# Four weight units read with a column step of 2, 4, 8 and 16 in a single-core encoder block

## The chip, the core and the metric

The kernel runs on one core of a Trainium2 chip. The metric is the device time of one execution in microseconds. It was 908.79 us before the change (median of two runs, 908.68 and 908.90).

## What is computed

One encoder block on 256 tokens of width 2048, in float32: a normed input projection into queries, keys, values and Fourier channels, windowed attention and a Fourier mix, an output projection, then a feed-forward part. Only the feed-forward part matters here:

```python
D_FF = ((8 * D_MODEL // 3 + 127) // 128) * 128      # 5504 = 43 tiles of 128
def _conv_ffn(h, w_up, dw_w, dw_b, w_down):
    up = h @ w_up                                   # (256, 2048) @ (2048, 11008)
    gate, val = up[..., :D_FF], up[..., D_FF:]
    gate = lax.conv_general_dilated(gate, dw_w, ...) + dw_b
    act = jax.nn.gelu(gate, approximate=False) * val
    return act @ w_down
```

## The kernel before

The kernel keeps float32 accuracy by writing each operand as the sum of a high and a low part, both in the fp32r format, and adding three products: high x high, low activation x high weight, high activation x low weight. The instruction order of every engine is written out by hand; nothing is rescheduled.

Weights come in *units*. A unit of the up-projection is one tile of 128 output columns, either of the gate or of the value half, over all 16 k tiles of the contraction: an SBUF tile of 128 partitions x 2048 elements, in which k tile k holds columns k*128 to k*128+127. One DMA of 1024 KB brings it (`load`, L183, three raw buffers), and two whole-row instructions split it (`split`): the scalar engine copies the high part (L191) and the vector engine subtracts for the low part (L192). The halves lie in one of three `parts` buffers.

`still_weights` then multiplies a unit. Weights are the stationary operand, so that each matmul has a weight load of 128 x 128 ahead of it (LDWEIGHTS in the profile, under PEld). For each of the 16 k tiles there are two matmuls: at L393 the high weights against the high and low activations, 512 columns, and at L395 the low weights against the high activations, 256 columns. The moving operand is read through `in_turn`, which takes one column from one half of the row and the next from the other half, 256 elements (1024 bytes) away:

```python
def in_turn(ap):
    return ap.rearrange("p (a e) -> p e a", a=2)
```

The main loop runs over `items`, an order fixed at build time. It begins with gate 0, value 0, gate 1, value 1, gate 2, value 2, gate 3, value 3; afterwards gate and value units alternate with products of the down-projection (`by_parts`, L1123 to L1125, matmuls of 512 columns). The last seven tiles are multiplied by `still_thirds` (L406, three matmuls of 256 columns for each k tile). After the two matmuls' sum is in PSUM, the scalar engine copies one half (L901) and the vector engine adds and scales (L902, L904); convolution, GELU and the product with the value follow one or two items later.

Two places in the kernel read SBUF with a step on other engines, and the prediction uses them. Values of late tiles are split with a step of 2 elements (L947 on the scalar engine, L948 on the vector engine, through `by_parity`), and the keys of the attention part with a step of 4 elements (L662 and L663):

```python
keys = add.rearrange("p (r a b) -> p a b r", a=2, b=2)
```

Of the kernel before, what the change touches and what calls it, by code (L numbers as in the profile page):

```python
# [13 lines left out]
P = 128  # L14
D = 2048
S = 256
NK = D // P
# [28 lines left out]
for _g in range(NKV):  # L46
# [21 lines left out]
}  # L68

PATTERNS = ["uuu" + "su" + "suu" * 6] + ["uuu" + "su" * 13 + "s"] * 3  # L70
PATTERNS += ["uuu" + "su" * 11 + "lslslsl"]
# [25 lines left out]
def block_kernel(  # L97
# [18 lines left out]
    nc = tc.nc  # L116
# [13 lines left out]
    def in_turn(ap):  # L130
        return ap.rearrange("p (a e) -> p e a", a=2)
# [17 lines left out]
    items, up_index = ff_items(), {}  # L149

    def in_thirds(j):

        return j >= LATE[0]
# [14 lines left out]
    raws, halves = {}, {}  # L168
# [59 lines left out]
    ps = bank(dn, "ps_warm")  # L228
# [19 lines left out]
    for c in range(4):  # L248
        t = base.tile([P, 4, 512], F32R, tag=f"hT{c}", name=f"hT{c}")
# [42 lines left out]
    k = 0  # L292
# [86 lines left out]
                ps, ah, wl, start=False, stop=last and q == q0 + len(kk) - 1  # L379
            )  # L380

    def still_weights(hi, lo, ps, kk, lag=0):


        todo = [("hi", k) for k in kk[: lag + 1]]
        for n, k in enumerate(kk):
            todo.append(("lo", k))
            todo += [("hi", q) for q in kk[lag + 1 + n : lag + 2 + n]]
        for part, k in todo:
            h = hT[k // 4][:, k % 4, :]  # L390
            s = slice(k * P, (k + 1) * P)
            if part == "hi":
                nc.tensor.matmul(ps, hi[:, s], in_turn(h), start=k == 0, stop=False)  # L393
            else:
                nc.tensor.matmul(  # L395
                    ps[:, 0:S], lo[:, s], in_turn(h)[:, 0:P], start=False, stop=k == NK - 1
                )

    def still_thirds(hi, lo, ps):
# [449 lines left out]
    for n, (c, kq) in enumerate(OUT_ORDER):  # L849
# [15 lines left out]
        if kq >= 2:  # L865
            part = "a" if kq == 2 else "f"
            ps = ps_a[c] if kq < 3 else ps_a[c, "f"]
# [315 lines left out]
    for q in range(2):  # L1183
        kind, j = items[q]
        ps = bank(mm, f"ps_{kind}{j}")
# [16 lines left out]
    for n, it in enumerate(items):  # L1202
        if n < 2:
            continue
        if it[0] == "last":
            break
        if n in (FIRST_PRODUCT - 9, FIRST_PRODUCT - 8):
            ring_load()
        if n == FIRST_PRODUCT - 6:
            pending.append(lambda: first_sums(*SETS[0]))  # L1210
        if it[0] in ("gate", "val"):
            kind, j = it
            ps = bank(mm, f"ps_{kind}{j}")
            if not in_thirds(j):
                still_weights(*halves.pop(up_index[n]), ps, range(NK), lag=4 if n == 2 else 0)
            else:
                still_thirds(*halves.pop(up_index[n]), ps)
            ff_step(n)
            up_posts(n, kind, j, ps)
            continue  # L1220
        if it[0] == "product":
            kind, g, c, p = it
            hi, lo = halves.pop(it)
            both = c == 2
            shape = (2, 1024) if both else (4, 512)
            for cc in (0, 1) if both else (c,):
                o = 512 * cc if both else 0
                if (cc, p) in held:
                    first, end = (g, c) == FIRST_SET[cc], (g, c) == LAST_SET[cc]
                    by_parts(held[cc, p], parts[p], hi, lo, first, end, *shape, o)  # L1230
                    continue
                ps = bank(mm, f"ps_{p}{g}{cc}")
                by_parts(ps, parts[p], hi, lo, True, True, *shape, o)
                at(beside, n + 1, product_out, g, cc, p, ps)
            if (g, c) == LAST_SET.get(c) and p == "P6":
                todo = shared_out(c)
                for m in (1, 3, 5):
                    at(behind, n + m, next, todo, None)
        else:
            kind, g, c = it  # L1240
            hi, lo = halves.pop(up_index[n])
            ps = [bank(mm, f"ps_l{g}{c}{b}") for b in range(2)]
            for b in range(2):
                moving_weights(hi, lo, 512, LATE, act.get, b, ps[b], True, True)
            at(beside, n + 1, down_out, c, ps)
            if (g, c) == (0, 0):
                gfb = base.tile([P, D], F32, tag="hT0", name="gfb")
                nc.gpsimd.dma_start(gfb, normf_g.partition_broadcast(P))
        ff_step(n)
# [53 lines left out]
def _layout(inp):  # L1303

    import numpy as np

    f = lambda a: np.ascontiguousarray(np.asarray(a), dtype=np.float32)
    x = f(inp["x"]).reshape(P, 2, D)
    by_parity = np.arange(S).reshape(P, 2).T.reshape(-1)

    def in_turn(w):

        return f(w).reshape(*w.shape[:-1], -1, 256, 2).swapaxes(-1, -2).reshape(w.shape)

    def tiles(v):
        return f(v).reshape(-1, P).T

    def moving(w, cols):

        return in_turn(w[:, cols]).reshape(-1, 4, P, cols.stop - cols.start).transpose(  # L1320
            0, 2, 1, 3
        ).reshape(-1, P, 4 * (cols.stop - cols.start))

    def still(w, c0):

        return f(w[:, c0 : c0 + P]).reshape(-1, P, P).transpose(1, 0, 2).reshape(1, P, -1)

    w_in = np.asarray(inp["w_in"])
    start = {"q": 0, "k": AW}
    kv = NKV * HD  # L1330
    win = np.concatenate(
        [moving(w_in, slice(AW + kv, AW + 2 * kv))]
        + [still(w_in, start[t] + h * HD) for t, h in QK_ORDER]
    )
    u0 = AW + 2 * kv
    u_rows = np.concatenate(
        [x.transpose(1, 0, 2).reshape(S, NK, P).transpose(2, 1, 0),
         in_turn(w_in[:, u0 : u0 + FW]).reshape(NK, P, FW).transpose(1, 0, 2)], axis=2,
    )
    w_out = np.asarray(inp["w_out"])  # L1340
    wout = np.concatenate(
        [moving(w_out, slice(c * 512, (c + 1) * 512))[k : k + 1] for c, k in OUT_ORDER]
    )
    w_up = np.asarray(inp["w_up"])
    wup = np.concatenate(
        [still(w_up, o + j * P) for j in range(NF) for o in (0, DFF)]
    )
    w_dn = np.asarray(inp["w_down"])
    def rows_by(tiles, cols, width=512):

        w = in_turn(w_dn[tiles[0] * P : (tiles[-1] + 1) * P, cols : cols + width])
        return w.reshape(len(tiles), P, width).transpose(1, 0, 2).reshape(P, -1)

    downs = []
    for g, c in SETS:
        half = len(GROUPS[g]) // 2
        width = 1024 if c == 2 else 512
        for k in (GROUPS[g][0], GROUPS[g][half]):
            for n in (0, 1024):
                downs.append(rows_by(range(k, k + half), n + (0 if c == 2 else 512 * c), width))  # L1360
    late = [rows_by(LATE, 512 * c) for c in range(4)]
    dw = f(inp["dw_w"]).reshape(3, NF, P).transpose(2, 1, 0).reshape(P, 3 * NF)
    sink = np.broadcast_to(f(inp["sink"])[None, :], (P, NH))
    vecs = np.concatenate(
        [tiles(inp["norm1_g"]), tiles(inp["norm2_g"]), tiles(inp["attn_out_g"]),
         tiles(inp["fourier_out_g"]), dw, tiles(inp["dw_b"]), sink], axis=1,
    )
    t = np.arange(S)
    ang = 2.0 * np.pi * ((t[:, None] * t[None, :]) % S) / S
    c_pos = np.concatenate(  # L1370
        [np.cos(ang[:, : S // 2 + 1]), np.sin(ang[:, 1 : S // 2])], axis=1
    )
    c_pos = c_pos[by_parity].reshape(2, P, P, 2).transpose(1, 3, 0, 2)
    k = np.arange(P)
    ang = 2.0 * np.pi * ((k[:, None] * k[None, :]) % P) / P
    c_chan = np.concatenate([np.cos(ang), -np.sin(ang)], axis=1) / np.sqrt(S * P)
    dist = np.abs(t[:, None] - t[None, :]).astype(np.float64)
    c_rel = np.where(dist <= WINDOW, dist, FAR)[by_parity][:, by_parity]
    c_rel = c_rel.reshape(2, P, S).transpose(1, 0, 2)
    return {  # L1380
        "x": x,
        "u_in": np.concatenate([tiles(inp["norm1_g"]), u_rows.reshape(P, -1)], axis=1),
        "vecs": np.ascontiguousarray(vecs),
        "wf": in_turn(f(inp["w_fourier"]).transpose(1, 0, 2).reshape(P, FW)),
        "w_in": win,
        "w_out": wout,
        "w_up": wup,
        "w_down": np.stack(downs),
        "w_down_late": np.stack(late),
        "w_down_last": np.stack([rows_by(LAST, 512 * c) for c in range(4)]),  # L1390
        "normf_g": f(inp["normf_g"]),
        "c_pos": np.ascontiguousarray(c_pos.reshape(P, 2 * S), dtype=np.float32),
        "c_chan": np.ascontiguousarray(c_chan, dtype=np.float32),
        "c_rel": np.ascontiguousarray(c_rel.reshape(P, 2 * S), dtype=np.float32),
    }
# [16 lines left out]
```

## Time and profile before

| | |
|---|---|
| time, median of two runs | 908.79 us |
| the profiled execution, its own time | 908.46 us |
| its span, first to last instruction | 906.7 us |
| TensorE matmul busy | 897.3 us (99%), 5299 instructions |
| TensorE weight load busy | 818.5 us (90%) |
| VectorE busy | 740.8 us (82%) |
| ScalarE busy | 545.6 us (60%) |
| granted TensorE clock | 0.998 |

In the profile PE is the matmul part of the tensor engine and PEld its weight loads, which overlap with the matmuls. Matmul rows overlap each other, since a row's duration includes the passage through the array; how long a matmul occupies the engine is read from the distance between starts. In rows of groups the columns are line, engine, operation, output and inputs, shape and count, then busy time and mean duration, then the idle time before them.

### The profile page before, as it was taken

How to read it: one execution, taken by the hardware profiler on the slowest of the kernel's cores; microseconds unless marked ns; L12 is line 12 of the kernel's file. 1: busy time of each engine (PE TensorE's matmuls, PEld its weight loads, DVE VectorE, ACT ScalarE, POOL GpSimd, SP SyncE). 2: the span in 40 equal slices, each digit the busy share in tenths (PEclk: the TensorE clock that was granted, in tenths of full speed). 3: DMA queues.
4: the chain of work that ended last, by engine and by line, in shares of the span. 5: the costliest groups of instructions: out<-in, count | busy, mean ns of one | idle time of the engine just before them, and what ended most of it. 6: DMA issues, size and time to landing. Idle time of an engine off the chain costs nothing.

```text
span 906.7 us, 13179 instructions
## 1 busy us (share of the span) xinstructions
PE 897.3 (99%) x5299; PEld 818.5 (90%) x5299; DVE 740.8 (82%) x879; ACT 545.6 (60%) x655; POOL 50.3 (6%) x64
## 2 busy tenths in 40 slices
PE   9999999999999999999999999999999999999996
PEld 8899999888899999999999999999999999999985
DVE  7579888676678877879887998888989789889796
ACT  7757777555455655556555575556655556655544
POOL 0001111000000000000000000000000000000003
PEclk9999999999999999999999999999999999999999
DMA  9874544446568687677898779787797978869742
GB/s 360 335 236 142 186 162 164 153 173 232 186 253 264 228 256 251 180 263 227 259 285 276 249 242 297 245 275 237 269 260 246 325 230 279 263 212 266 234 186 93
DMA packets 32765, 214.88 MB, mean 237 GB/s; under 512 B 3616, under 2 KB 3872, under 8 KB 8384
## 3 DMA queue, kind: packets, MB, share of 16 engines
q1 hardware_dynamic: 28592, 184.55, 54.4%
q0 software_dynamic: 4112, 29.49, 17.2%
q8 instruction: 41, 0.67, 0.3%
q14 instruction: 20, 0.16, 0.0%
HBM read 211.93 MB, written 2.10 MB: 236 GB/s over the span
## 4 chain that ended last, share of the span: by engine, by line
PE 90%; DMA 4%; issue 3%; POOL 1%; DVE 1%; ACT 0%; SPq 0%; ACTq 0%; POOLq 0%
PE ps_val L393 14%; PE ps_gate L393 14%; PE ps_gate L395 7%; PE ps_val L395 7%; PE ps_q L393 5%; PE ps_gate L406 4%; PE ps_val L406 4%; PE ps_P L1123 3%; PE ps_P L1125 3%; PE ps_P L1124 3%; PE ps_N L1123 2%; PE ps_N L1125 2%; PE ps_N L1124 2%; PE ps_q L395 2%; PE ps_a L376 2%
## 5 line engine op out<-in xcount | busy, mean ns | idle before, releaser
L192 DVE TENSOR_TENSOR parts<-raw,parts 128x2048 fp32r<-128x2048 f32 (+1 forms) x129 | 293.3, 2273 | 52.4 <-ACT parts L191 51.9
L191 ACT ACTIVATE parts<-raw 128x2048 fp32r<-128x2048 f32 (+1 forms) x129 | 245.5, 1903 | 48.9 <-PE ps_a L378 12.4
L393 PE MATMUL ps_val<-hU,parts 128*128 128x512 f32 x576 | 190.7, 382 | 0.0
L393 PE MATMUL ps_gate<-hU,parts 128*128 128x512 f32 x576 | 190.2, 382 | 0.0
L395 PE MATMUL ps_val<-hU,parts 128*128 128x256 f32 x576 | 157.0, 273 | 0.0
L395 PE MATMUL ps_gate<-hU,parts 128*128 128x256 f32 x576 | 156.4, 273 | 0.0
L393 PEld LDWEIGHTS ps_val<-hU,parts 128*128 128x128 f32 x576 | 108.9, 189 | 15.2
L393 PEld LDWEIGHTS ps_gate<-hU,parts 128*128 128x128 f32 x576 | 108.8, 189 | 15.2
L395 PEld LDWEIGHTS ps_val<-hU,parts 128*128 128x128 f32 x576 | 110.5, 192 | 0.6
L395 PEld LDWEIGHTS ps_gate<-hU,parts 128*128 128x128 f32 x576 | 110.3, 192 | 0.8
L901 ACT ACTIVATE ft_g<-ps_gate 128x256 f32<-128x256 f32 x36 | 13.8, 384 | 98.8 <-PE ps_gate L395 96.2
L393 PE MATMUL ps_q<-hT,parts 128*128 128x512 f32 x192 | 62.6, 384 | 0.0
L1123 PE MATMUL ps_P<-parts_P,op_P 128*128 128x512 f32 x144 | 54.7, 380 | 0.0
L1124 PE MATMUL ps_P<-parts_P,op_P 128*128 128x512 f32 x144 | 54.6, 379 | 0.0
L1125 PE MATMUL ps_P<-parts_P,op_P 128*128 128x512 f32 x144 | 54.6, 379 | 0.0
L901 ACT ACTIVATE ft_v<-ps_val 128x256 f32<-128x256 f32 x36 | 13.8, 384 | 63.1 <-PE ps_val L395 63.1
L395 PE MATMUL ps_q<-hT,parts 128*128 128x256 f32 x192 | 50.4, 273 | 0.0
L1009 DVE TENSOR_TENSOR parts_N<-sumw,parts_N 128x2048 fp32r<-128x2048 f32 x18 | 41.2, 2289 | 10.2 <-ACT parts_N L1008 10.2
L1123 PE MATMUL ps_N<-parts_N,op_N 128*128 128x512 f32 x108 | 41.0, 380 | 0.0
L1124 PE MATMUL ps_N<-parts_N,op_N 128*128 128x512 f32 x108 | 40.9, 379 | 0.0
L1125 PE MATMUL ps_N<-parts_N,op_N 128*128 128x512 f32 x108 | 40.9, 379 | 0.0
L393 PEld LDWEIGHTS ps_q<-hT,parts 128*128 128x128 f32 x192 | 36.1, 189 | 4.7
(350 smaller groups left out, 1707.3 us busy)
## 6 DMA issues: line engine op xcount, KB each, us to landing
raw<-in_w_up SPq DMA_DIRECT2D x86, 1024.0 KB, 6.0
raw<-in_w_in SPq DMA_DIRECT2D x20, 1024.0 KB, 5.9
sumw<-in_w_down POOLq DMA_DIRECT2D x18, 1024.0 KB, 8.6
raw<-in_w_out SPq DMA_DIRECT2D x16, 1024.0 KB, 4.8
raw<-in_w_down_late SPq DMA_DIRECT2D x4, 1024.0 KB, 6.0
u_raw<-in_u_in SPq DMA_DIRECT2D x4, 768.0 KB, 10.4
raw<-in_w_down_last SPq DMA_DIRECT2D x4, 768.0 KB, 4.2
u_raw<-in_u_in SPq DMA_DIRECT2D x7, 384.0 KB, 6.0
```

What stands on the lines that cost most here:

```text
L191: nc.scalar.activation(hi, raw, AF.Copy)
L192: nc.vector.tensor_tensor(lo, raw, f32(hi), ALU.subtract)
L376: nc.tensor.matmul(ps, ah, wh, start=first and q == q0, stop=False)
L393: nc.tensor.matmul(ps, hi[:, s], in_turn(h), start=k == 0, stop=False)
L395: nc.tensor.matmul(ps[:, 0:S], lo[:, s], in_turn(h)[:, 0:P], start=False, stop=k == NK - 1)
L406: nc.tensor.matmul(ps[:, 0:S], w[:, s], in_turn(h)[:, part * P : (part + 1) * P], start=k == 0 and n == 0, stop=k == NK - 1 and n == 2,)
L901: nc.scalar.activation(tmp, ps[:, S : 2 * S], AF.Copy)
L1009: nc.vector.tensor_tensor(lo, src, f32(hi), ALU.subtract)
L1123: nc.tensor.matmul(ps, o[:, 0, p, :], wh, start=first and p == 0, stop=False)
L1124: nc.tensor.matmul(ps, o[:, 1, p, :], wh, start=False, stop=False)
L1125: nc.tensor.matmul(ps, o[:, 0, p, :], wl, start=False, stop=end)
```

## The change

A table `STEPS` names four units and a step for each: gate 2 with 2, value 2 with 4, gate 3 with 8, value 3 with 16. For these units the host lays the columns of `step` neighbouring k tiles out in turn: first column 0 of each of them, then column 1 of each, and so on. `columns` gives a matmul the 128 columns of k tile k as a slice with that step. The values that are multiplied, the order of the products and the size of every transfer are the same; the other 82 gate and value units have step 1. In the changed kernel the two matmuls stand at L401 and L403.

```diff
+STEPS = {("gate", 2): 2, ("val", 2): 4, ("gate", 3): 8, ("val", 3): 16}
...
+    def columns(t, k, step):
+
+        o = k // step * step * P + k % step
+        return t[:, o : o + step * (P - 1) + 1 : step]
+
-    def still_weights(hi, lo, ps, kk, lag=0):
+    def still_weights(hi, lo, ps, kk, lag=0, step=1):
...
         for part, k in todo:
             h = hT[k // 4][:, k % 4, :]
-            s = slice(k * P, (k + 1) * P)
+            w = columns(hi if part == "hi" else lo, k, step)
             if part == "hi":
-                nc.tensor.matmul(ps, hi[:, s], in_turn(h), start=k == 0, stop=False)
+                nc.tensor.matmul(ps, w, in_turn(h), start=k == 0, stop=False)
             else:
                 nc.tensor.matmul(
-                    ps[:, 0:S], lo[:, s], in_turn(h)[:, 0:P], start=False, stop=k == NK - 1
+                    ps[:, 0:S], w, in_turn(h)[:, 0:P], start=False, stop=k == NK - 1
                 )
...
-                still_weights(*halves.pop(up_index[n]), ps, range(NK), lag=4 if n == 2 else 0)
+                still_weights(
+                    *halves.pop(up_index[n]), ps, range(NK), lag=4 if n == 2 else 0,
+                    step=STEPS.get((kind, j), 1),
+                )
...
+    for (kind, j), step in STEPS.items():
+        w = wup[2 * j + (kind == "val")]
+        w[:] = w.reshape(P, -1, step, P).swapaxes(2, 3).reshape(P, -1)
```

## The prediction

> **What bounds the kernel now.** I read the page's busy shares first, then the chain that ended last, then the costliest groups, then the busy time by stretch for the four units that change.
>
> ```profile
> span 906.7 us, 13179 instructions
> PE 897.3 (99%) x5299; PEld 818.5 (90%) x5299; DVE 740.8 (82%) x879; ACT 545.6 (60%) x655; POOL 50.3 (6%) x64
> ...
> PE 90%; DMA 4%; issue 3%; POOL 1%; DVE 1%; ACT 0%; SPq 0%; ACTq 0%; POOLq 0%
> ...
> L393 PE MATMUL ps_gate<-hU,parts 128*128 128x512 f32 x576 | 190.2, 382 | 0.0
> L395 PE MATMUL ps_gate<-hU,parts 128*128 128x256 f32 x576 | 156.4, 273 | 0.0
> L393 PEld LDWEIGHTS ps_gate<-hU,parts 128*128 128x128 f32 x576 | 108.8, 189 | 15.2
> L395 PEld LDWEIGHTS ps_gate<-hU,parts 128*128 128x128 f32 x576 | 110.3, 192 | 0.8
> ```
>
> The tensor engine is the bound and its weight loads are busy beside it almost all the time: the load row of L393 has 15.2 us of idle before it over 576 loads, that of L395 only 0.8. So in a gate or value unit one of the two loads of a k tile is tight. The four units that change are gate 2, value 2, gate 3 and value 3, the fifth to eighth units of the up-projection. They follow one another without a gap:
>
> ```profile
> core 0: us, PE busy (x) PEld busy (x) DVE busy (x) ACT busy (x) POOL busy (x), PEclk, DMA share, GB/s
> 266.94:272.18 5.24, 5.24 (x35) 4.82 (x34) 4.83 (x6) 3.47 (x6) 0.00 (x0) 1.00 1.00 408
> 272.18:277.42 5.24, 5.24 (x35) 4.82 (x34) 4.29 (x6) 2.67 (x3) 0.00 (x0) 1.00 0.75 283
> 277.42:282.66 5.24, 5.24 (x35) 4.82 (x34) 5.21 (x6) 2.61 (x3) 0.94 (x1) 1.00 0.86 245
> 282.66:287.90 5.24, 5.24 (x35) 4.82 (x34) 3.89 (x6) 2.67 (x3) 0.00 (x0) 1.00 0.97 228
> 287.90:500.00 212.10, 212.10 (x1225) 192.87 (x1224) 175.19 (x181) 124.76 (x131) 6.96 (x8) 1.00 0.78 249
> 500.00:700.00 200.00, 200.00 (x1136) 181.28 (x1135) 176.81 (x175) 122.38 (x119) 8.75 (x10) 1.00 0.81 257
> 700.00:890.00 190.00, 190.00 (x1252) 176.75 (x1252) 164.65 (x158) 108.81 (x98) 7.61 (x10) 1.00 0.76 241
> ```
>
> Two things are to be seen. Each unit takes 5.24 us, which is 5.24 / 16 = 327.5 ns for one k tile (one high matmul of 512 columns at L393 and one low matmul of 256 at L395). And from 287.90 to 890.00 the tensor engine never stands still, so there is no later wait that could swallow a delay: what these four units lose arrives at the end in full, and no other engine gets work that it did not have.
>
> Now the inside of a k tile. The matmul rows overlap, so starts are to be compared, not durations:
>
> ```profile
> 500.20 0.38 PE L1123 MATMUL ps_P<-parts_P,op_P 128*128 128x512 f32 x1
> 500.41 0.38 PE L1124 MATMUL ps_P<-parts_P,op_P 128*128 128x512 f32 x1
> 500.63 0.38 PE L1125 MATMUL ps_P<-parts_P,op_P 128*128 128x512 f32 x1
> ...
> 266.94 0.38 PE L393 MATMUL ps_gate<-hU,parts 128*128 128x512 f32 x1
> 267.15 0.27 PE L395 MATMUL ps_gate<-hU,parts 128*128 128x256 f32 x1
> ...
> 266.94 0.19 PEld L395 LDWEIGHTS ps_gate<-hU,parts 128*128 128x128 f32 x1
> 267.16 0.19 PEld L393 LDWEIGHTS ps_gate<-hU,parts 128*128 128x128 f32 x1
> ...
> 764.91 1.31 PEld L406 LDWEIGHTS ps_gate<-hU,parts 128*128 128x128 f32 x11
> ```
>
> A matmul of 512 columns occupies (500.63 - 500.20) / 2 = 215 ns; I take 216. A load starts together with the matmul before the one it serves (266.94 with 266.94, 267.16 with 267.15), so only one load is ahead, and a slot lasts as long as the longer of matmul and load. Eleven loads in a row at L406, behind 256-column matmuls, take 1.31 us: (1310 - 192) / 10 = 112 ns each, of which I call 111.5 the load's occupancy, because 216 + 111.5 gives the 327.5 measured. Hence the model used below, for a load of X ns: one k tile costs max(216, X) + max(111.5, X). The high slot has 104 ns to spare, the low slot none.
>
> **The change part by part.** Removed and added: no instruction. The order of every engine's instructions is the same in number and kind, so no wait, no transfer and no queue moves. The host arranges the four units' columns differently; the transfers stay 1024 KB each, and the split into halves (L191, L192) still reads and writes whole contiguous rows, so its durations stay. These parts cost nothing because nothing in them changes, not because something hides them. What changes is the address pattern of 4 x 32 = 128 weight loads: consecutive columns lie 2, 4, 8 or 16 elements (8, 16, 32, 64 bytes) apart.
>
> The trace has no weight load with a step; the contiguous ones of these lines last 189 and 192 ns (rows above). The nearest rows are the scalar and vector engines' reads of the same memory with steps: L529/L530 contiguous, L947/L948 in steps of 2, L662/L663 in steps of 4 (each with 256 elements).
>
> ```profile
> L275 ACT ACTIVATE parts<-u_raw 128x1024 fp32r<-128x1024 f32 x4 | 4.2, 1044 | 0.0
> L191 ACT ACTIVATE parts<-raw 128x2048 fp32r<-128x2048 f32 x126 | 241.1, 1913 | 40.8 <-PE ps_a L378 12.4 <-PE ps_ff L378 9.1 <-PE ps_P L1125 6.5
> L529 ACT ACTIVATE chan_hl<-chan 128x256 fp32r<-128x256 f32 x1 | 0.4, 407 | 0.0
> L947 ACT ACTIVATE act<-fa_v 128x256 fp32r<-128x256 f32 x7 | 3.5, 502 | 4.7 <-DVE fa_v L935 4.7
> L662 ACT ACTIVATE kT<-add_k 128x256 fp32r<-128x256 f32 x4 | 3.4, 854 | 8.7 <-DVE add_k L649 8.7
> ...
> L276 DVE TENSOR_TENSOR parts<-u_raw,parts 128x1024 fp32r<-128x1024 f32 x4 | 4.9, 1223 | 0.5 <-ACT parts L275 0.5
> L192 DVE TENSOR_TENSOR parts<-raw,parts 128x2048 fp32r<-128x2048 f32 x126 | 288.0, 2286 | 52.4 <-ACT parts L191 51.9
> L530 DVE TENSOR_TENSOR chan_hl<-chan,chan_hl 128x256 fp32r<-128x256 f32 x1 | 0.4, 423 | 0.0
> L948 DVE TENSOR_TENSOR act<-fa_v,act 128x256 fp32r<-128x256 f32 x7 | 3.3, 473 | 0.0
> L663 DVE TENSOR_TENSOR kT<-add_k,kT 128x256 fp32r<-128x256 f32 x4 | 3.3, 816 | 3.7 <-ACT kT L662 3.7
> ```
>
> Scalar engine: (1913 - 1044) / 1024 = 0.85 ns an element, so 407 - 256 x 0.85 = 190 ns is fixed. Step 2 is then (502 - 190) / 256 = 1.22 ns, step 4 (854 - 190) / 256 = 2.59 ns. Vector engine: (2286 - 1223) / 1024 = 1.04 ns, 157 ns fixed; step 2 is (473 - 157) / 256 = 1.23 ns, step 4 (816 - 157) / 256 = 2.57 ns. Two engines of different speed agree on 1.23 and 2.58, so this looks like the memory: about 2.5 ns for every 16 bytes newly touched, whether two elements or one are taken from them. A contiguous weight load, 111.5 / 128 = 0.87 ns a column, sits close to the scalar engine's 0.85.
>
> By these rows a load with step 2 takes 111.5 + 128 x (1.23 - 0.85) = 160 ns and one with step 4 takes 111.5 + 128 x (2.58 - 0.85) = 333 ns; steps 8 and 16 I put at the same 333, since there too each column has its 16 bytes to itself.
> - Gate 2 (step 2): the high slot still covers the load (160 under 216), the low slot grows by 160 - 111.5 = 48.5 ns; times 16, +0.8 us.
> - Value 2, gate 3, value 3: (333 - 216) + (333 - 111.5) = 338.5 ns a k tile; times 16, +5.4 us each, +16.2 us for three.
> - Sum: +17.0 us. On the profiled execution's 908.46 us that is 925.5; its time lies 0.33 us below the median of 908.79, so I forecast **925.8 us**, or +1.9%.
>
> The bounds of this one unknown. From below: a matmul's moving operand alternates between two places 1024 bytes apart (in_turn), so each column is in other bytes than the one before, and yet the rows at L1123 to L1125 give 216 / 512 = 0.42 ns a column. The tensor engine therefore keeps at least two places open; a load that did so perfectly would cost nothing. A gain is excluded, almost: a faster load could shorten only the low slot, from 111.5 to half of 216, or 64 x 3.5 = 0.2 us in all four units. From above the rows give no end for 32 and 64 bytes; I take a doubling of 2.58 for the widest. I take 333 rather than 111.5 because the load is the nearer kin of the other engines' reads: one stream, one element after another, at their rate, not at the 0.42 ns of the moving read.
>
> A rule that bears on it: the Trainium skill, "SBUF — State Buffer", specifications and the note on cachelines, says that a line has 16 bytes, that two hits in a line are needed for full bandwidth and that a read which goes to a new line each time pays. By it step 2 would be free and the sum 16.2 instead of 17.0. The rows agree on the break at 16 bytes (2.58 ns), not quite on step 2 (1.22 against 0.85 ns), and the moving read at 0.42 ns contradicts the rule's plain form.
>
> **The rivals.**
> - *The step costs nothing (not slower).* Place: the load's read, if it keeps several 16-byte pieces in flight as the moving read does. For it: 0.42 ns a column above. Against it: two engines that pay alike. It holds while X stays at 111.5, and the time is **908.8**. The Trainium skill, "TensorE: Matmul & The Clock Gate", section on loading the stationary operand, speaks for it: a load there costs its columns divided by 1.2 GHz, without a word on their step (107 ns for 128, near the 112 here).
> - *Two pieces in flight.* The load pays half of 2.58, or 1.29 ns a column: step 2 is covered by 0.85, the others take 111.5 + 128 x 0.44 = 168 ns, 56 ns more in the low slot only; 48 k tiles x 56 = +2.7 us, **911.5**. A plain halving of the load's rate (X = 223) would be 48 x (7 + 111.5) = +5.7, 914.5.
> - *The wider steps cost more than 16 bytes do.* Pieces 64 bytes apart may fall on a part of the memory that is still busy with the one before, or with the moving read. If value 3 pays 5.16 ns a column, X is 111.5 + 128 x 4.31 = 663, its k tile grows by 447 + 551.5 ns, 16 us instead of 5.4: **936.4**. For it: the 16-byte rows already show no overlap of one fetch with the next. Against it: no row with a wider step. It decides the verdict from X = 345 ns as a mean of the three units: (48 x (690 - 327.5)) = 17.4, with 0.8 that is 2% of 908.79.
>
> **How the numbers follow.** Forecast case 0.40, free 0.14, two in flight 0.17, wider steps dearer 0.27, a gain from something unseen 0.02. The forecast's own range is 923 to 929 (2.45 to 2.65 ns a piece). Two per cent, about what a measurement of this kernel can tell from no change, lies at 927.0, inside that range: of the forecast's 0.40 I put half beyond it. So faster 0.02, within 2% 0.20 + 0.14 + 0.17 = 0.51, slower 0.20 + 0.27 = 0.47. The range reaches down to the free case, 908.5, and up to 940, a little beyond the doubled widest step; above it some 0.12 stay out.
>
> **What would show it.** In the changed kernel's profile: the same counts on every engine; the group of loads at the matmuls of L401 and L403 split, with 32 loads near 240 ns (192 + 48.5) and 96 near 415; the four stretches 6.0, 10.7, 10.7 and 10.7 us long instead of 5.24; all other stretches as before, and the clock still at 1.00 there. Four stretches of 5.24 us show the free case, 6.1 for the last three two pieces in flight, lengths that rise with the step the third rival. The model of the slots is wrong if loads lengthen and the stretches do not by that much; the whole argument is wrong if anything outside these four units moves by more than 1 us.

## The result and the profile after

The changed kernel takes **915.59 us** (median of two runs, 915.42 and 915.76) against 908.79 before: a ratio of 1.0073, 95% interval 1.0057 to 1.009, or +6.80 us. The forecast was 925.8, +17.0 us. It had the sign right and the size two and a half times too large.

The page of the changed kernel, in the same order as before: span, busy shares, chain, then the groups of the two matmul lines' loads.

```profile
span 914.0 us, 13179 instructions
...
PE 904.7 (99%) x5299; PEld 827.6 (91%) x5299; DVE 740.9 (81%) x879; ACT 545.2 (60%) x655; POOL 50.2 (5%) x64
...
L401 PEld LDWEIGHTS ps_val<-hU,parts 128*128 128x128 f32 x576 | 113.1, 196 | 14.3
L401 PEld LDWEIGHTS ps_gate<-hU,parts 128*128 128x128 f32 x576 | 111.3, 193 | 14.6
L403 PEld LDWEIGHTS ps_val<-hU,parts 128*128 128x128 f32 x576 | 114.9, 200 | 0.6
L403 PEld LDWEIGHTS ps_gate<-hU,parts 128*128 128x128 f32 x576 | 112.7, 196 | 0.8
```

Every count is what it was, and the vector and scalar engines are as busy as before (740.9 and 545.2 us against 740.8 and 545.6). Only PE and PEld grew, by 7.4 and 9.1 us. A mean of 200 ns over 576 loads hides that 32 of them are far longer; the stretches show it. The next view is the busy time by stretch: the four changed units, one after the other with steps 2, 4, 8 and 16, then the rest.

```profile
core 0: us, PE busy (x) PEld busy (x) DVE busy (x) ACT busy (x) POOL busy (x), PEclk, DMA share, GB/s
267.41:272.74 5.33, 5.33 (x34) 5.06 (x33) 4.94 (x6) 3.47 (x6) 0.00 (x0) 1.00 1.01 423
272.74:280.33 7.59, 7.59 (x35) 7.59 (x33) 6.57 (x8) 2.67 (x3) 0.00 (x0) 1.00 0.80 266
280.33:288.02 7.69, 7.69 (x35) 7.69 (x33) 3.31 (x4) 2.49 (x3) 0.94 (x1) 1.00 0.95 209
288.02:295.22 7.20, 7.20 (x34) 7.20 (x33) 4.02 (x5) 2.67 (x3) 0.00 (x0) 1.00 0.57 189
295.22:700.00 404.78, 404.78 (x2318) 367.54 (x2317) 344.37 (x347) 242.03 (x244) 14.81 (x17) 1.00 0.79 251
700.00:897.00 197.00, 197.00 (x1291) 183.08 (x1290) 171.50 (x165) 113.45 (x101) 8.41 (x10) 1.00 0.77 241
```

The four stretches take 5.33, 7.59, 7.69 and 7.20 us instead of 5.24 each: 0.09 + 2.35 + 2.45 + 1.96 = 6.85 us more, against 6.80 between the medians. (The two profiled executions are 7.3 us apart; the other 0.47 us lies ahead of the changed units, whose first start also moves between 266.94 and 267.65 us in traces of kernels that are alike up to there.) In the last three the weight load is busy for the whole stretch: there it is the bound, where before its rows left 0.42 us idle in each unit. From 295.22 to 897.00 the tensor engine never stands still, so nothing gave the delay back. The widest step is not the dearest.

With the prediction's slots, max(216, X) + max(111.5, X) for one k tile, the stretches give the load's occupancy X: 5.33 / 16 = 333.4 ns, so X = 117; 7.59 / 16 = 474, X = 237; 7.69 / 16 = 481, X = 240; 7.20 / 16 = 450, X = 225. The timeline of the step-4 unit shows the same directly (start and duration in us):

```profile
273.08 0.33 PEld L401 LDWEIGHTS ps_val<-hU,parts 128*128 128x128 f32 x1
273.32 0.34 PEld L403 LDWEIGHTS ps_val<-hU,parts 128*128 128x128 f32 x1
273.56 0.33 PEld L401 LDWEIGHTS ps_val<-hU,parts 128*128 128x128 f32 x1
273.80 0.34 PEld L403 LDWEIGHTS ps_val<-hU,parts 128*128 128x128 f32 x1
...
273.21 0.50 PE L401 MATMUL ps_val<-hU,parts 128*128 128x512 f32 x1
273.55 0.30 PE L403 MATMUL ps_val<-hU,parts 128*128 128x256 f32 x1
273.69 0.51 PE L401 MATMUL ps_val<-hU,parts 128*128 128x512 f32 x1
```

Loads start every 0.24 us, whether a 512-column or a 256-column matmul is ahead of them; before, they started 0.22 and 0.11 us apart in turn. The matmul rows are longer than before (0.50 and 0.30 against 0.38 and 0.27) although their work is the same. Why the rows stretch is not shown, and the distances between starts account for the time without it.

### The profile page after: what moved, and what is told of

It is laid out like the page before. It is cut to its first block, busy times and chain, and to the rows that moved or that the text cites. A ratio compares the mean times of both kernels' runs of the same rounds, so it can differ in the third digit from the quotient of the medians.

```text
span 914.0 us, 13179 instructions
## 1 busy us (share of the span) xinstructions
PE 904.7 (99%) x5299; PEld 827.6 (91%) x5299; DVE 740.9 (81%) x879; ACT 545.2 (60%) x655; POOL 50.2 (5%) x64
## 4 chain that ended last, share of the span: by engine, by line
PE 94%; issue 3%; DMA 1%; POOL 1%; DVE 1%; ACT 0%; POOLq 0%; ACTq 0%
PE ps_val L401 14%; PE ps_gate L401 14%; PE ps_val L403 7%; PE ps_gate L403 7%; PE ps_q L401 5%; PE ps_gate L414 4%; PE ps_val L414 4%; PE ps_P L1131 3%; PE ps_P L1132 3%; PE ps_P L1133 3%; PE ps_N L1131 2%; PE ps_N L1132 2%; PE ps_N L1133 2%; PE ps_u L290 2%; PE ps_q L403 2%
## 5 line engine op out<-in xcount | busy, mean ns | idle before, releaser
L401 PE MATMUL ps_val<-hU,parts 128*128 128x512 f32 x576 | 195.0, 388 | 0.0
L401 PE MATMUL ps_gate<-hU,parts 128*128 128x512 f32 x576 | 192.7, 386 | 0.0
L403 PE MATMUL ps_val<-hU,parts 128*128 128x256 f32 x576 | 157.6, 274 | 0.0
L403 PE MATMUL ps_gate<-hU,parts 128*128 128x256 f32 x576 | 156.8, 273 | 0.0
L401 PEld LDWEIGHTS ps_val<-hU,parts 128*128 128x128 f32 x576 | 113.1, 196 | 14.3
L401 PEld LDWEIGHTS ps_gate<-hU,parts 128*128 128x128 f32 x576 | 111.3, 193 | 14.6
L403 PEld LDWEIGHTS ps_val<-hU,parts 128*128 128x128 f32 x576 | 114.9, 200 | 0.6
L403 PEld LDWEIGHTS ps_gate<-hU,parts 128*128 128x128 f32 x576 | 112.7, 196 | 0.8
L401 PE MATMUL ps_q<-hT,parts 128*128 128x512 f32 x192 | 62.6, 384 | 0.0
L403 PE MATMUL ps_q<-hT,parts 128*128 128x256 f32 x192 | 50.4, 273 | 0.0
L401 PEld LDWEIGHTS ps_q<-hT,parts 128*128 128x128 f32 x192 | 36.1, 189 | 4.7
```

The costliest lines, as they stand in the source:

```text
L401: nc.tensor.matmul(ps, w, in_turn(h), start=k == 0, stop=False)
L403: nc.tensor.matmul(ps[:, 0:S], w, in_turn(h)[:, 0:P], start=False, stop=k == NK - 1)
```

## The experiments

**Theory A**, made after the result, keeps the slots and changes the price: a load pays about 1.8 ns for each 16 bytes that it newly touches, never less than its contiguous 0.85 ns a column. Experiments 1, 2, 3, 5, 6 and 7 share one edit: each unit has a step for its high and one for its low weights, a number of places among which the moving read goes round, and a flag for short moving operands.

```diff
-    def still_weights(hi, lo, ps, kk, lag=0, step=1):
+    def columns(t, k, way):
+        o = k // way * way * P + k % way if 16 % way == 0 else k
+        return t[:, o : o + way * (P - 1) + 1 : way]
+    def still_weights(hi, lo, ps, kk, lag=0, spec=None):
+        hw, lw, mv, short = spec or (1, 1, 2, False)
...
+            w = columns(hi, k, hw) if part == "hi" else columns(lo, k, lw)
+            m = h if mv == 1 else h.rearrange("p (a e) -> p e a", a=mv)
...
```

**1. Many steps, and one half alone.** Two units for each way, from tile 2 on.

```diff
+WAYS = [(s, s, 2, False) for s in (1, 2, 3, 4, 5, 6, 7, 8, 9, 10, 12, 14, 16)]
+WAYS += [(4, 1, 2, False), (1, 4, 2, False), (16, 1, 2, False), (1, 16, 2, False)]
```

> Steps 1 to 10, 12, 14 and 16 in gate and value units from tile 2 on, two units each, then units in which only the high or only the low weights have the step (4 and 16). The host layout is the contiguous one, so these units multiply columns of other k tiles; the time of a k tile is what is read. In the result, unit lengths of 5.33, 7.59, 7.69 and 7.19 us gave 333, 474, 481 and 449 ns a k tile for steps 2, 4, 8, 16; with slots max(216, X) + max(111.5, X) that is a load X of 117, 237, 240 and 225 ns. Theory A (one 16-byte piece at a time, 1.8 ns each, only in the load): X = 3 + 128 x max(0.85, 1.8 x pieces per column), so a k tile takes 328 ns at step 1, 334 at 2, 392 at 3 (three pieces for four columns) and 467 for every step from 4 on, odd ones too. Theory B (the place in memory matters: pieces collide with the moving read or with each other by their distance): from 4 on the time varies with the step by more than 5%, odd steps differ from even ones, 4, 8 and 16 stay as in the result. Halves: by the slot model a step of 4 on the high weights alone gives 216 + 237 = 453 ns (its load lies in the short slot), on the low weights alone 237 + 111.5 = 348; a rival in which each strided load costs the same wherever it lies gives 401 for both.

The whole takes 965.0 us (one run). The stretches below hold 14 k tiles of one unit each, so a row divided by 14 is a k tile. In order: steps 1, 2, 3, 4, 8, then 12 (the whole unit, 16 k tiles), 16, then step 4 on the high weights alone and on the low weights alone.

```profile
core 0: us, PE busy (x) PEld busy (x) DVE busy (x) ACT busy (x) POOL busy (x), PEclk, DMA share, GB/s
267.98:272.57 4.59, 4.59 (x31) 4.23 (x29) 4.25 (x6) 3.15 (x5) 0.00 (x0) 1.00 1.00 418
278.47:283.14 4.67, 4.67 (x30) 4.42 (x29) 4.63 (x5) 2.53 (x3) 0.94 (x1) 1.00 0.96 260
289.20:294.68 5.48, 5.48 (x30) 5.48 (x29) 3.44 (x4) 2.67 (x4) 0.00 (x0) 1.00 0.79 293
301.80:308.45 6.65, 6.65 (x30) 6.65 (x29) 3.86 (x5) 2.28 (x3) 0.00 (x0) 1.00 0.52 182
373.17:379.90 6.73, 6.73 (x30) 6.73 (x29) 4.48 (x3) 2.56 (x3) 0.00 (x0) 1.00 0.58 174
423.25:431.84 8.59, 8.59 (x34) 8.59 (x33) 3.68 (x4) 3.01 (x4) 0.00 (x0) 1.00 0.46 175
461.32:467.62 6.30, 6.30 (x30) 6.30 (x29) 6.16 (x6) 2.30 (x2) 0.86 (x1) 1.00 0.42 70
480.69:487.00 6.31, 6.31 (x31) 5.94 (x29) 5.01 (x4) 1.77 (x1) 0.87 (x1) 1.00 0.44 70
500.07:504.92 4.85, 4.85 (x30) 4.85 (x29) 4.85 (x4) 1.77 (x1) 0.00 (x0) 1.00 0.00 0
```

In ns a k tile: 328, 334, 391, 475, 481, 537, 450, then 451 and 346. Steps 1 to 3 fall on theory A's formula; X is 112, 118 and 176 there, that is 0.87, 0.92 and 1.37 ns a column for 4, 8 and 12 bytes. From step 4 on it levels off, not quite evenly: 237, 225, 224, 234, 241, 241, 231, 242 and 225 at steps 4, 5, 6, 7, 8, 9, 10, 14 and 16, and 268 at step 12, which no theory here explains. Theory A had 467 ns a k tile for all of these; 449 to 484 were measured, and 537 at step 12. By the expectation's own terms a spread above 5% speaks for theory B, so that experiments 2, 3 and 5 had to decide between the two. The two halves settle the slots: a 237 ns load costs 237 - 216 = 21 ns behind the long matmul and 237 - 111.5 = 125 ns behind the short one; 19 and 123 were measured. The low weights' load starts with the long matmul, so the *low* weights with a step cost little.

**2. Loads alone.** The same steps with a moving operand of 32 columns in k tiles 1 to 14, so that only the load can fill a slot (the products of the other columns are left out). The edit is shown against experiment 1.

```diff
-WAYS = [(s, s, 2, False) for s in (1, 2, 3, 4, 5, 6, 7, 8, 9, 10, 12, 14, 16)]
+WAYS = [(s, s, 2, True) for s in (1, 2, 3, 4, 5, 6, 7, 8, 9, 10, 12, 14, 16)]
```

> The same steps, but in these units the matmuls of k tiles 1 to 14 have a moving operand of 32 columns only, so that the load is bare and the moving read nearly gone; those units compute only part of their sums. A k tile then takes 2 X. Theory A: 2 X = 223 ns at step 1, 236 at 2, 352 at 3, 467 from 4 on: the same X as under full matmuls. Theory B: bare loads with wide steps are clearly faster than 237 ns each, 2 X below 430 at steps 4, 8 and 16, and the irregularity between steps goes away. Third possibility: loads in the prediction's size, 333 ns each (2 X = 666), which the long matmuls hid in part.

It takes 985.72 us, longer than with the full matmuls, for a reason of its own. The stretches hold 11 k tiles, or 22 loads, of the first step-1 unit, the first step-2 unit and the first step-4 unit; the third number from the right is the granted clock:

```profile
core 0: us, PE busy (x) PEld busy (x) DVE busy (x) ACT busy (x) POOL busy (x), PEclk, DMA share, GB/s
267.43:269.89 2.46, 2.46 (x26) 2.46 (x24) 2.29 (x5) 2.46 (x4) 0.00 (x0) 1.00 1.01 423
277.91:282.60 4.69, 4.69 (x23) 4.69 (x24) 3.92 (x6) 1.86 (x2) 0.94 (x1) 0.50 0.92 252
306.94:312.10 5.16, 5.16 (x23) 5.16 (x24) 3.59 (x5) 1.85 (x2) 0.00 (x0) 0.50 0.29 79
```

Before the clock fell, a contiguous load took 2.46 / 22 = 112 ns. Then the clock went to 0.50, and a step-2 load took 4.69 / 22 = 213 ns, though experiment 1 has it at 118. A step-4 load took 235 ns, against 237 at full clock. So the price of step 4 is the same in nanoseconds at half the granted clock, and the moving read, almost gone here, has no part in it. For steps 2 and 3 the experiment decided nothing: both took 213 at the halved clock.

**3. The moving read.** Weights contiguous and the moving read over 1 to 128 places; then steps 4 and 16 with some of these.

```diff
+WAYS = [(1, 1, m, False) for m in (1, 2, 4, 8, 16, 32, 64, 128)]
+WAYS += [(4, 4, m, False) for m in (1, 2, 4, 16, 128)] + [(16, 16, m, False) for m in (1, 2, 128)]
```

> Other moving reads, two units each. First contiguous weights with the activations read from 1 (plain order), 2 (as the kernel does), 4, 8, 16, 32, 64 and 128 places in turn (128 places: neighbouring columns 16 bytes apart); then weights with step 4 and with step 16 under some of these. Outputs come in another order of tokens, and where the plain order differs the sums too; the time of a k tile is what is read. Theory A with the moving read working as the load does (1.8 ns a piece): the plain order takes 0.45 ns a column, 230 + 115 = 345 ns a k tile; 2 places 327.5; and 128 places 1.8 ns a column, 922 + 461 = 1383. With weights at step 4 a k tile stays at 474 under all moving reads that are themselves fast. Theory B: the moving read changes the load: step 4 with the plain order or with another number of places differs from 474 by more than 5%. If the moving read keeps many pieces open, all eight orders take 327.5.

One run, 1025.65 us. Fourteen k tiles each: contiguous weights with the moving read in plain order, in two places, in four and in 128 (each column 16 bytes from the one before); then step-4 weights with plain order and with two places.

```profile
core 0: us, PE busy (x) PEld busy (x) DVE busy (x) ACT busy (x) POOL busy (x), PEclk, DMA share, GB/s
267.47:272.23 4.76, 4.76 (x31) 4.21 (x29) 4.31 (x6) 3.13 (x5) 0.00 (x0) 1.00 1.01 417
278.33:282.92 4.59, 4.59 (x31) 4.22 (x30) 4.55 (x6) 2.54 (x3) 0.94 (x1) 1.00 0.90 252
288.90:294.77 5.87, 5.87 (x30) 4.60 (x29) 3.39 (x4) 2.64 (x4) 0.00 (x0) 1.00 0.77 275
401.82:411.52 9.70, 9.70 (x29) 5.82 (x28) 4.13 (x3) 2.25 (x2) 0.00 (x0) 1.00 0.62 216
426.29:432.88 6.59, 6.59 (x31) 6.59 (x29) 5.66 (x5) 1.75 (x1) 0.00 (x0) 1.00 0.45 159
443.82:450.48 6.66, 6.66 (x30) 6.66 (x29) 5.68 (x5) 1.75 (x1) 0.00 (x0) 1.00 1.01 283
```

Plain order costs 340 ns a k tile, two places 328, four places 419, 128 places 693. With step-4 weights it is 471 in plain order and 476 in two places: the moving read's order hardly touches the load. Step-4 weights under 4, 16 and 128 places, timed in the same trace over whole units, take 508, 669 and 702 ns, and the slots, with the matmuls as long as under contiguous weights, give 516, 673 and 699. So the rival in which the two reads get in each other's way falls. Theory A did not fit the moving side: it had 1383 ns for 128 places, and 693 / 768 = 0.90 ns a column is half of 1.8. Nor is the number of places the whole story: 8 places took 737 ns, 16, 32 and 64 places 654, 652 and 649. Why is not shown.

**4. The other engines at wider steps.** The kernel before, with one scalar copy and one vector subtraction more for each late unit, on its raw weights with a step (the other probes have 128 elements, or the blocked order of the keys):

```diff
+PROBES = [(256, 1, "one"), (256, 2, "two"), (256, 3, "three"), (256, 4, "four"), (256, 8, "eight")]
...
+        r = raw[:, 0 : s * (n - 1) + 1 : s]
...
+        nc.scalar.activation(a, r, AF.Copy)
+        nc.vector.tensor_tensor(b, r, hi, ALU.subtract)
```

> The kernel before, with one extra scalar-engine copy and one extra vector-engine subtraction after each split of a gate or value unit from tile 2 on; they read the raw weights with a step and their result goes nowhere. 256 elements with steps 1, 2, 3, 4, 8; 128 elements with steps 1, 4, 8, 12, 16; and 256 elements in the order of the keys of the attention part (blocks of 64 with step 4), the form from which 2.58 ns an element was taken. Theory A (the price of a 16-byte piece belongs to the reading engine: 2.58 ns on these two, 1.8 ns in the weight load): steps 4 and 8 cost 2.58 ns an element, the scalar engine 850 ns for 256 elements and 520 for 128, the vector engine 816 and 487. Theory B (2.58 ns came from the blocked order, and the memory's price is 1.8 ns for everyone): only the blocked form lasts 850 and 816 ns; the plain step 4 takes 190 + 256 x 1.8 = 650 on the scalar engine and 157 + 461 = 618 on the vector engine. Either: step 16 differs from 4 by less than a fifth, as in the weight load.

The groups of the added lines, one scalar and two vector ones shown against their neighbours (256 elements each, mean ns after the comma):

```profile
L216 ACT ACTIVATE p_one<-raw 128x256 f32<-128x256 f32 x7 | 2.8, 404 | 0.0
L216 ACT ACTIVATE p_two<-raw 128x256 f32<-128x256 f32 x7 | 3.6, 510 | 0.0
L216 ACT ACTIVATE p_four<-raw 128x256 f32<-128x256 f32 x6 | 5.1, 847 | 0.0
L216 ACT ACTIVATE p_eight<-raw 128x256 f32<-128x256 f32 x6 | 4.0, 666 | 0.0
...
L217 DVE TENSOR_TENSOR p_four<-raw,parts 128x256 f32<-128x256 f32 x6 | 4.9, 815 | 0.0
L217 DVE TENSOR_TENSOR p_eight<-raw,parts 128x256 f32<-128x256 f32 x6 | 3.7, 619 | 0.0
```

This is where the prediction's price came apart. Step 4 costs (847 - 190) / 256 = 2.57 ns an element on the scalar engine and (815 - 157) / 256 = 2.57 on the vector engine, as the prediction had read. But step 8 costs only 1.86 and 1.80. Neither recorded theory had that: one put step 8 at 2.58 too, the other gave 2.58 to the keys' blocked order alone, which took 873 and 809 ns, about as long as the plain step 4. It looked as if going on to the *neighbouring* 16 bytes cost 2.57 and a jump beyond them 1.8, which experiment 8 tests. Shorter probes agree (128 elements on the scalar engine: 527 ns at step 4, 422 to 427 at steps 8, 12 and 16).

**5. Loads alone, spread out.** As 2, but only in one unit of four, so that the clock holds through steps 1 to 3.

```diff
+WAYS = [(s, s, 2, True) for s in (1, 2, 3, 4, 8, 12, 16)]
...
+SPEC = {u: WAYS[n // 4 % 7] for n, u in enumerate(UNITS) if n % 4 == 0}
```

> Bare loads again (moving operand of 32 columns in k tiles 1 to 14, so that part of the sums is left out), but in one unit of four only, so that the granted clock should stay at 1.00; steps 1, 2, 3, 4, 8, 12, 16. With the clock halved the bare loads took 213 ns at steps 1 to 3 and 234, 238, 268, 217 ns at 4, 8, 12, 16. Theory A (the load's own 16-byte price, X = 3 + 128 x max(0.85, 1.8 x pieces per column)): 112, 118, 176 ns at steps 1, 2, 3 and again 234, 238, 268, 217 at the others, since the price is in nanoseconds and not in clocks of the tensor engine. Theory B (a part of the price is waiting for the moving read): step 3 below 165 and step 4 below 220 with the clock at full rate.

One run, 947.5 us; 22 loads a row, steps 1, 2, 3, 4 and 16:

```profile
core 0: us, PE busy (x) PEld busy (x) DVE busy (x) ACT busy (x) POOL busy (x), PEclk, DMA share, GB/s
267.61:270.06 2.45, 2.45 (x25) 2.45 (x24) 2.29 (x5) 2.45 (x4) 0.00 (x0) 1.00 1.01 425
288.80:291.39 2.59, 2.59 (x26) 2.59 (x24) 1.04 (x2) 2.56 (x4) 0.00 (x0) 1.00 1.03 383
313.77:317.65 3.88, 3.88 (x24) 3.88 (x24) 3.77 (x4) 2.58 (x3) 0.00 (x0) 1.00 0.72 251
341.99:347.17 5.18, 5.18 (x24) 5.18 (x24) 5.18 (x5) 1.35 (x1) 0.00 (x0) 0.83 0.53 180
430.79:435.57 4.78, 4.78 (x23) 4.78 (x24) 4.78 (x6) 2.22 (x2) 0.87 (x1) 0.85 0.56 185
```

The bare loads take 111, 118, 176, 235 and 217 ns; beside full matmuls experiment 1 gave 112, 118, 176, 237 and 225. Up to step 4 the load has its price by itself, within 2 ns; the 8 ns at step 16 no run explains. Step 12 is as dear bare as in experiment 1, 269 ns in the same trace. Step 3 shows the rule: three of four columns open a new piece there, 0.75 x 1.8 x 128 = 173.

**6 and 7. One half of the change.** The four units of the change with the steps on the high weights alone, and on the low weights alone, five runs and eleven. The first line is experiment 6, the second experiment 7.

```diff
+SPEC = {u: (s, 1, 2, False) for u, s in STEPS.items()}
+SPEC = {u: (1, s, 2, False) for u, s in STEPS.items()}
```

> The four units with their steps 2, 4, 8, 16 on the high weights alone; the low weights are read contiguously, and the host layout is the contiguous one, so the high products of these units take columns of other k tiles. The load of a high tile lies in the slot of the low matmul of 256 columns. Slot model with the k-tile times of the first experiment (333, 450, about 452, 435 against 327.5 ns): 0.1 + 2.0 + 2.0 + 1.7 = 5.8 us, 914.6. Rival (each strided load costs the same, 6.8 us for 128 of them): 3.4 us, 912.2.

> The same steps on the low weights alone; the low products of these units take columns of other k tiles. Their loads lie in the slot of the high matmul of 512 columns, 216 ns. Slot model (327.5, 346.5, about 349, 336 ns): 0 + 0.3 + 0.35 + 0.15 = 0.8 us, 909.6. Rival (each strided load costs the same): 3.4 us, 912.2.

High only: 914.88 us against 908.77, ratio 1.0068 (1.0055 to 1.008), +6.1 us. Low only: 909.52, ratio 1.0009 (1.0 to 1.0018), +0.75 us. The same steps cost some eight times as much behind the short matmul as behind the long one; the factor is rough, since the second interval reaches from 0 to 1.6 us. The two sum to 6.85, the whole change.

**8. Backwards.** Experiment 4's probes with negative steps, and with steps 5 and 6.

```diff
+PROBES = [(256, 4, "four"), (256, -4, "back_four"), (256, -1, "back_one"), (256, -2, "back_two")]
+PROBES += [(256, -3, "back_three"), (256, 5, "five"), (256, 6, "six"), (256, -8, "back_eight")]
```

> Extra reads on the scalar and vector engine as before, 256 elements, now with steps 4, 5, 6 forwards and 1, 2, 3, 4, 8 backwards. So far: step 4 forwards cost 2.57 ns an element, step 8 1.8; in the weight load both cost 1.8. Theory C (2.57 is the price of going up to the next 16 bytes, a collision of neighbours in that direction): steps 5 and 6, which jump over a piece only now and then, lie between 1.8 and 2.57 forwards, and backwards step 4 costs 1.8, 650 ns on the scalar engine and 618 on the vector engine, step 3 190 + 256 x 0.75 x 1.8 = 536 and step 2 about 420. Theory D (neighbouring pieces cost 2.57 on these two engines in either direction): backwards as forwards, 847 and 815 ns at step 4, 682 at 3, 510 at 2. Step 8 backwards 666 and 619 in both.

The groups of the added lines:

```profile
L210 ACT ACTIVATE p_four<-raw 128x256 f32<-128x256 f32 x9 | 7.5, 839 | 0.0
L210 ACT ACTIVATE p_back_four<-raw 128x256 f32<-128x256 f32 x9 | 6.1, 681 | 0.0
L210 ACT ACTIVATE p_five<-raw 128x256 f32<-128x256 f32 x8 | 5.5, 694 | 0.0
...
L211 DVE TENSOR_TENSOR p_four<-raw,parts 128x256 f32<-128x256 f32 x9 | 7.1, 786 | 0.0
L211 DVE TENSOR_TENSOR p_back_four<-raw,parts 128x256 f32<-128x256 f32 x9 | 5.7, 630 | 0.0
```

On both engines step 4 is dear only upwards: 839 against 681 ns downwards, 786 against 630. But steps 5 and 6 speak against the reading of experiment 4. At step 5 three of four elements still go on to the next 16 bytes, at step 6 every second one; with 2.57 and 1.86 that gives 802 and 757 ns on the scalar engine, and 694 and 681 were measured, near the 666 of step 8 in experiment 4. So the extra price is shown for steps 3 and 4 upwards and not for neighbouring pieces as such; its cause stays open. The load's own prices by step (0.9, 1.4, 1.85, 1.9 ns a column at 2, 3, 4 and 8) have the shape of the scalar engine's backward reads (0.97, 1.44, 1.92, 1.96 from 438, 558, 681 and 692 ns), not of its forward ones (1.25, 1.92, 2.57, 1.86 in experiment 4). That a load takes its columns from the last to the first would explain it; no run here shows that it does.

**9. Step 2 everywhere.** All 70 units of tiles 1 to 35, with the host's order to match.

```diff
-STEPS = {("gate", 2): 2, ("val", 2): 4, ("gate", 3): 8, ("val", 3): 16}
+STEPS = {(kind, j): 2 for j in range(1, 36) for kind in ("gate", "val")}
```

> The change with step 2 in all 70 gate and value units that take the argument (tiles 1 to 35), and no wider step. If two columns in each 16 bytes are free, the time is that of before. By the 333.4 ns a k tile of the changed kernel's step-2 unit against 327.5, 70 x 16 x 5.9 ns = 6.6 us, 915.4, provided that the tensor engine carries each delay to the end.

915.53 us against 908.6, ratio 1.0076 (1.0059 to 1.0092), +6.9 us. That is 6.9 / (70 x 16) = 6.2 ns a k tile, the 6 of experiment 1 carried to the end in full through 1120 k tiles.

## Why the prediction was right or wrong

- *The bound and the slots: right.* One load ahead, one k tile max(216, X) + max(111.5, X). Experiments 1, 6 and 7 measured its two terms apart (123 and 19 ns a k tile at step 4, 6.1 and 0.75 us in all).
- *Nothing else moves, and the delay arrives in full: right.* The four stretches are 6.85 us longer, 6.80 were measured in all, the clock is 1.00 in them, and experiment 9 shows the same for a delay spread over the whole main loop.
- *Step 4: the term was mis-sized, and this is the step that failed.* "One with step 4 takes 111.5 + 128 x (2.58 - 0.85) = 333 ns" measured 237, which makes a unit 2.35 us longer and not 5.4. The reading of the rows was sound (experiment 4 repeats 2.57); the inference "this looks like the memory", from two engines that agreed, was not. The two engines agree at step 4 upwards, for a cause that stays open; at wider steps or backwards they pay 1.8 to 2.0 ns for a new piece. The load pays 1.85 ns a column at step 4 and 1.75 to 1.9 at the wider steps, but for step 12 with 2.1.
- *Steps 8 and 16 "at the same 333": wrong by the same price*, 240 and 225 measured. Even for the two engines the rows were taken from it did not hold: their step 8 is cheaper than their step 4.
- *Step 2 at 160 ns: wrong in size, harmless.* It measured 117, +0.09 us for the unit instead of +0.8. Two elements from each piece are 0.9 ns a column, just above the contiguous 0.87. The rule weighed there, of the Trainium skill, "SBUF — State Buffer" (its note on cachelines, two hits for full bandwidth), comes close for the load, where the trace leaves 6 ns of 328, and fails for the scalar engine's upward read, 510 against 404 ns in experiment 4.
- With 1.8 in place of 2.58 the same working gives X = 111.5 + 128 x (1.8 - 0.85) = 233 and 48 x (17 + 121.5) = 6.65, and 0.1 for gate 2: 6.75 us, against 6.80 measured. The 1.8 was taken from the result itself, so this confirms the slots and the sum, not the price; for the price, experiments 1 and 5 stand.
- *The range: mis-added.* "2.45 to 2.65 ns a piece" gives 924.2 to 926.7 us by the prediction's own sum, not "923 to 929". So 927.0 lies just outside, and half of the forecast's chance beyond it does not follow.
- *The rivals.* The free step falls: 237 ns, not 111.5, at step 4. The Trainium skill, "TensorE: Matmul & The Clock Gate", section on loading the stationary operand, has a load at its columns over 1.2 GHz, with no word on their step; the 107 ns of that are near the contiguous 112 here and not the 237. Two pieces in flight, with X = 168, falls for the load; the moving read's 0.90 ns a column would fit it. The aside "a plain halving of the load's rate", X = 223 and 914.5 us, came within 1.1 us; it had no mechanism behind it, and X is 237, 240 and 225, so its nearness is in part luck. Dearer wide steps fall: 16 is cheaper than 8, and only 12 stands out, by 27 ns over 8.
- *What stays open:* why step 12 takes 268 ns and the other wide steps scatter from 224 to 242, what makes steps 3 and 4 upwards dearer than 5 and more on the other two engines, and why the load's step 4 lacks that extra price.

## What to carry to other kernels

A strided weight load costs only what it exceeds the matmul ahead of it: a load that opens a new 16 bytes for each column takes some 225 to 242 ns here instead of 112 (268 at step 12), which at step 4 cost 19 ns behind 512 moving columns and 123 ns behind 256, so put the strided operand where the matmul ahead is long. Two float32 elements from each 16 bytes are nearly free for the load (6 ns of 328, which still came to 6.9 us over all 70 units), so an interleave of two is cheap and one of four is not. A price taken from other engines' rows need not hold even for the same step (2.57 ns there, 1.85 in the load): probe one more step, the other direction and the engine itself before calling it the memory's.

## What was not expected of the hardware

- A step-2 weight load is slower at half the granted clock (118 ns at 1.00, 213 at 0.50), a step-4 load is not (237 and 235).
- With units of short matmuls one after another the granted clock was 1.00 in the first, 0.59 in the second and 0.50 in the third (experiment 2); with one such unit in four it was 0.76 to 1.00 in them (experiment 5).
- The moving operand is read faster from two places in turn than in plain order (328 against 340 ns a k tile), more slowly from four (419), and slowest of the eight orders from eight (737).
- Reading every fourth float32 backwards is faster than forwards on the scalar and vector engines, 681 against 839 ns and 630 against 786 ns.
